# Seven products for up blocks 7, 8, 9, 11, 12, 13 and 14 of a fused transformer block, and one buffer each for gates and values

## The chip, the core and the metric

The kernel runs on one core of one Trainium2 chip. The metric is the device time of one execution, in microseconds (us). Blocks are counted from 0, as in the code.

## What is computed

One layer on a sequence of 512 tokens and 1024 features, in 32-bit floats: a normalisation, an mLSTM and a sparse attention side by side, an output projection, a feed-forward part with a short convolution, a gated embedding, and a last normalisation. The change touches the feed-forward part alone:

```python
def conv_ffn(h, w_up, conv_w, conv_b, w_down):
    u = h @ w_up                                   # 512x1024 by 1024x4096
    gate, val = jnp.split(u, 2, axis=-1)           # 2048 features each
    gate = conv(gate, conv_w) + conv_b             # three taps along the tokens, feature by feature
    return (jax.nn.silu(gate) * val) @ w_down      # 512x2048 by 2048x1024
...
x = x + conv_ffn(rms_norm(x, ln2_g[i]), w_up[i], conv_w[i], conv_b[i], w_down[i])
```

## The kernel before

Every product of 32-bit numbers is made of three: each operand is split into a high part (ScalarE copies it to the rounded type, line 205) and a low part (VectorE subtracts, line 209), and high by high, low by high and high by low are added up in PSUM. Names ending in `r`, `h` and `l` are the raw, high and low tile of one set of weights.

The 2048 features of the feed-forward part are 16 up blocks of 128. Features lie on the partitions, the 512 tokens along the free dimension. An **ordinary** block has two jobs, `wu80` (gate) and `wu81` (value): in each, eight slices of 128 input features by three products of 512 columns go into one bank. The gate is convolved (`convolve`, tile `cv`: one ScalarE and two VectorE instructions, then Silu), the value multiplied by it (tile `zv`), and the result split into `U` for the down products (`hidden`, lines 1224 and 1225).

A block in the table `FAST` takes the 2x2 product of gate and value halves by halves of the tokens and of the input features with seven half-sized products instead of eight. Its four jobs are `wu90`, `wu9s`, `wu9t` and `wu91`, with two, two, two and one of the seven products; each of these is twelve matmuls of 256 columns (`seven`, lines 1273 to 1277). What it needs beside them: GpSimd makes four sums of the raw weights (lines 1314 to 1318, in two rooms of the tile `ws`), which are split for jobs `s` and `t`; and VectorE adds the seven results together (lines 1340 to 1364, tiles `fu`, `fv`, `zg`, `zv`). The banks of such blocks change between two sets.

Weights are loaded on SyncE's queue and split by a stream of jobs: with `st.depth = 2` and `st.ahead = 3` two jobs are split and three more loaded ahead, in a ring of three raw, three high and three low tiles, so the high part of a job may be written only when TensorE has done the job three places before. The instructions of each engine run in the order of the program that a scheduler makes of these jobs. GpSimd's first sum for a block is put behind the latest clearing of a gate's margin:

```python
i = GE.tensor_add(s1, raw[:, 0:4], raw[:, 4:8])
behind(i, zeroed[0], "not long in front of its block")
GE.tensor_sub(s2, s1, r0[:, 0:4])
GE.tensor_sub(s3, r0[:, 0:4], raw[:, 0:4])
GE.tensor_sub(s4, r0[:, 4:8], s2)
```

Before, blocks 7, 9, 10, 12 and 13 are in the table; 8, 11, 14 and 15 are ordinary, and so are blocks 0 to 6. Blocks 0 to 4 are evacuated with the norm's factors (`rb2`) while the scaled input is made (`scaled_input`, with GpSimd sums of its own, lines 1261 to 1264).

Of the kernel before, what the change touches and what calls it, by code (L numbers as in the profile page):

```python
# [7 lines left out]
F32 = mybir.dt.float32  # L8
I32 = mybir.dt.int32
F32R = mybir.dt.float32r  # L10
# [5 lines left out]
S = 512  # L16
# [25 lines left out]
T_QK = 2.0  # L42
T_NR = 3.2
LASTW = 256
FAST = (7, 9, 10, 12, 13)
UNSCALED = 5
T_XN = 0.4, 4.9
T_TS = 2.0, 4.5
# [25 lines left out]
def f32(ap):  # L74
    return ap.bitcast(F32)
# [3 lines left out]
def hybrid_block_kernel(ctx: ExitStack, tc: tile.TileContext, a, out):  # L79
# [26 lines left out]
    def pV(name):  # L106
        return bank("V", 1, 1, name)
# [7 lines left out]
    def t2k(name, dt=F32):  # L115
        return tmp.tile([128, 512], dt, tag="t2k", name=name)
# [102 lines left out]
    def behind(later, sooner, why, wait=False):  # L219
        kind = mybir.DependencyClass.Sync if wait else mybir.DependencyClass.NoSync  # L220
        tc.add_manual_dep(later.ins, sooner.ins.name, mybir.DependencyInfo(kind, mybir.DependencyReason.DATA),
                          reason=why)
# [955 lines left out]
    def start_norm(norm, acc, name):  # L1178
        def stats():
            if norm is n3:  # L1180
                norm["yc"] = rstd_stats(acc, name)
                return
            ah, al = (fpool.tile([128, S], F32R, tag="zv", name=name + c) for c in "hl")
            SE.activation(ah, acc, AF.Copy)
            VE.tensor_sub(al, acc, f32(ah))
            st.after(T_NR, lambda: rows(ah, al))

        def rows(ah, al):

            ps = pV(name + "ps")  # L1190
            TE.matmul(ps, onesr, ah, start=True, stop=False)
            TE.matmul(ps, onesr, al, start=False, stop=True)
            v, y = t2k(name + "v"), t2k(name + "y")
            rb = tmp.tile([128, 512], F32, tag="rb", bufs=1, name=name + "rb")
            VE.tensor_scalar(v, ps, 1.0 / D, EPS, op0=ALU.mult, op1=ALU.add)
            SE.activation(y, v, AF.Abs_reciprocal_sqrt)
            VE.tensor_mul(rb, y, y)
            VE.scalar_tensor_tensor(rb, rb, -0.5, v, op0=ALU.mult, op1=ALU.mult)
            VE.scalar_tensor_tensor(rb, rb, 1.5, y, op0=ALU.add, op1=ALU.mult)
            norm["rb"] = rb  # L1200
            for fn in norm.get("pending", []):
                fn()
            for q, b in enumerate((0, 4, 1, 5, 2, 6, 3, 7)):
                st.after(T_XN[0] + T_XN[1] * q, lambda b=b: scaled_input(b))
        st.after(T_NS, stats)

    def gate_rows(f):
        zg = fpool.tile([128, S + 2], F32, name=f"zg{f}", tag="zg")
        zeroed[0] = GE.memset(zg[:, 0:2], 0.0)  # L1209
        return zg  # L1210

    def convolve(f, zg):
        cw = lambda j: cols[:, C_CW + 16 * j + f:C_CW + 16 * j + f + 1]
        cv = fpool.tile([128, S], F32, name=f"cv{f}", tag="cv")
        SE.activation(cv, zg[:, 2:S + 2], AF.Identity, scale=cw(2), bias=cols[:, C_CB + f:C_CB + f + 1])  # L1215
        VE.scalar_tensor_tensor(cv, zg[:, 1:S + 1], cw(1), cv, op0=ALU.mult, op1=ALU.add)  # L1216
        VE.scalar_tensor_tensor(cv, zg[:, 0:S], cw(0), cv, op0=ALU.mult, op1=ALU.add)  # L1217
        SE.activation(cv, cv, AF.Silu)  # L1218
        n2["cv"] = cv

    def hidden(f, zv):
        if f == max(FAST):
            U.room(range(f, 16), main.tile([128, 2, 4, S], F32R, tag="XH", name="u3"))
        SE.activation(U[0][:, f], zv, AF.Copy)  # L1224
        VE.tensor_sub(U[1][:, f], zv, f32(U[0][:, f]))  # L1225

    def up_evac(f, part, ps, rb2):

        if part == 0:
            zg = gate_rows(f)  # L1230
            if rb2 is None:
                SE.activation(zg[:, 2:S + 2], ps, AF.Copy)
            else:
                VE.tensor_mul(zg[:, 2:S + 2], ps, rb2)  # L1234
            convolve(f, zg)
        else:
            zv = fpool.tile([128, S], F32, name=f"zv{f}", tag="zv")
            if rb2 is None:
                VE.tensor_mul(zv, ps, n2["cv"])
            else:  # L1240
                VE.tensor_mul(zv, ps, rb2)
                VE.tensor_mul(zv, zv, n2["cv"])  # L1242
            hidden(f, zv)
# [53 lines left out]
    def up_fast(f):  # L1297
        d = {}
        half = lambda w, q: (w[0][:, 4 * q:4 * q + 4], w[1][:, 4 * q:4 * q + 4])

        def landed_a(raw):
            d["r0"] = raw

        def landed_b(raw):
            r0, d["r1"] = d["r0"], raw
            if not rooms:
                rooms.append(fpool.tile([128, 2, 8, 128], F32, bufs=1, name="ws", tag="xturn"))
                rooms.append(0)
            sums = []
            for _ in range(2):  # L1310
                sums.append(rooms[0][:, rooms[1] % 2])
                rooms[1] += 1
            s2, s1, s3, s4 = sums[0][:, 0:4], sums[0][:, 4:8], sums[1][:, 0:4], sums[1][:, 4:8]
# [5 lines that stand above are left out]
            d["sums"] = sums  # L1319

        def prep_b(name, raw, shape):
            return split(name, d["sums"][0], shape)

        def prep_c(name, raw, shape):
            return split(name, d["sums"][1], shape)

        def prep_d(name, raw, shape):
            return split(name, d["r1"][:, 4:8], shape)

        def run_a(wh, wl):  # L1330
            d["ps"] = fast_banks(f)
            d["u"] = t2k(f"fu{f}")
            d["v"] = t2k(f"fv{f}")
            p1, p2 = d["ps"][0:2]
            yield from seven(p1, half((wh, wl), 0), quarter(0, 0))
            v1 = d["v"][:, H:]
            yield from seven(p2, half((wh, wl), 1), quarter(4, 0))
            SE.activation(v1, p1, AF.Copy)
            d["zg"] = gate_rows(f)
            VE.tensor_add(d["zg"][:, 2:2 + H], p2, v1)  # L1340

        def run_b(wh, wl):
            p1, p2, p6, p5 = d["ps"][0:4]
            u2, u4 = d["u"][:, 0:H], d["v"][:, 0:H]
            yield from seven(p6, half((wh, wl), 0), tsum(1))
            yield from seven(p5, half((wh, wl), 1), tsum(0))
            VE.tensor_add(u2, p6, d["v"][:, H:])
            VE.tensor_add(u4, p5, u2)

        def run_c(wh, wl):  # L1350
            p5, p7, p3 = d["ps"][3:6]
            u2, u3, u4 = d["u"][:, 0:H], d["u"][:, H:], d["v"][:, 0:H]
            d["zv"] = fpool.tile([128, S], F32, name=f"zv{f}", tag="zv")
            yield from seven(p7, half((wh, wl), 0), tsum(2))
            yield from seven(p3, half((wh, wl), 1), quarter(4, H))
            VE.tensor_add(d["zg"][:, 2 + H:], p3, u4)
            convolve(f, d["zg"])
            VE.tensor_add(u3, p7, u2)
            VE.tensor_add(d["zv"][:, H:], p5, u3)

        def run_d(wh, wl):
            zv, p4 = d["zv"], d["ps"][6]
            yield from seven(p4, (wh, wl), tsum(3))
            VE.tensor_add(zv[:, 0:H], p4, d["u"][:, H:])
            VE.tensor_mul(zv, zv, n2["cv"])
            hidden(f, zv)

        full = [128, KB, 128]
        st.add(f"wu{f}0", a["w_up"][:, f, 0], full, run_a, landed=landed_a)
        st.add(f"wu{f}s", a["w_up"][:, f, 1], full, run_b, prep_b, landed_b)  # L1370
        st.add(f"wu{f}t", None, full, run_c, prep_c)
        st.add(f"wu{f}1", None, [128, 4, 128], run_d, prep_d)

# [33 lines left out]
    for f in range(16):  # L1407
        if f in FAST:
            up_fast(f)
# [5 lines left out]
    fpool = ctx.enter_context(tc.tile_pool(name="fpool", bufs=2))  # L1415
    U = Parts()
# [9 lines left out]
    for j in range(4):  # L1426
        st.after(T_TS[0] + T_TS[1] * j, lambda j=j: split_sums(j))
    st.until(f"wu{min(FAST) - 2}1")
    st.depth, st.ahead = 2, AHEAD
    st.until("wu71")  # L1430
    U.room(range(8, 12), main.tile([128, 2, 4, S], F32R, tag="B16", bufs=3, name="u2"))
    U.room((12,), fpool.tile([128, 2, 1, S], F32R, bufs=1, name="u12"))
    st.until(f"wu{max(FAST)}1")
    st.depth, st.ahead = 1, 0
    st.until("wu151")
# [114 lines left out]
    for t in range(NT):  # L1550
# [3 lines left out]
        for part, (c0, c1) in enumerate(cuts):  # L1554
            if part:
                ps = pG("pg1last")
            for k in range(KB):
# [5 lines left out]
                if part == 0 and k == 5:  # L1563
                    VE.tensor_mul(xo[:, t, 0], xo[:, t, 0], gF[:, 0])
                    f = 1.0 if t < NT - 1 else -0.5
# [101 lines left out]
```

## Time and profile before

| | |
|---|---|
| median of 3 runs | 622.81 us (622.48 to 622.87) |
| the profiled execution, its own time | 622.97 us |
| its span, first to last instruction | 621.2 us |
| TensorE (PE) busy | 609.9 us, 98% |
| VectorE (DVE) busy | 452.3 us, 73% |
| ScalarE (ACT) busy | 338.9 us, 55% |
| GpSimd (POOL) busy | 113.4 us, 18% |

Busy shares are averages over stages that differ; the up blocks in question lie between 386.9 and 480.9 us. The two digits rows of the page say how busy an engine is in 40 slices of some 15.5 us each.

### The profile page before, as it was taken

What the parts mean: (1) busy time and instruction counts of PE and PEld (TensorE: products, weight loads), DVE (VectorE), ACT (ScalarE), POOL (GpSimd) and SP (SyncE); (2) the same over time, 40 slices, a digit from 0 to 9 for tenths busy, and PEclk for the clock granted to TensorE, in tenths of its full rate; (3) what the DMA queues carried; (4) which work ended last, traced back from release to release, by engine and by line L of the source; (5) the groups of instructions that cost most, each with busy time, mean ns of one, the idle gap of its engine ahead of it and who ended that gap; (6) DMA issues with size and microseconds to landing.
All of it is one profiled execution on the core that took longest, in us unless ns stands there. A gap on an engine that the chain in (4) does not pass through costs nothing.

```text
span 621.2 us, 8920 instructions
## 1 busy us (share of the span) xinstructions
PE 609.9 (98%) x3195; PEld 505.1 (81%) x3195; DVE 452.3 (73%) x842; ACT 338.9 (55%) x700; POOL 113.4 (18%) x169
## 2 busy tenths in 40 slices
PE   8999999999999999999999999999999999999994
PEld 6888877777777778887878888999998888888784
DVE  5988847787877778883879997979794435355376
ACT  7556556777767766654656564554563223242254
POOL 0400009332333500000003624253500000000000
PEclk9999999999999999999999999999999999999998
DMA  8722035212211233022232332423232332634703
GB/s 309 284 74 85 19 118 144 61 35 68 70 43 60 77 128 102 35 59 79 69 102 88 108 109 102 137 72 132 78 127 68 102 100 78 161 102 145 192 4 135
DMA packets 23212, 63.07 MB, mean 102 GB/s; under 512 B 2744, under 2 KB 7736, under 8 KB 23100
## 3 DMA queue, kind: packets, MB, share of 16 engines
q1 hardware_dynamic: 21632, 59.93, 29.8%
q0 software_dynamic: 1248, 2.16, 1.5%
q8 instruction: 25, 0.41, 0.3%
q10 hardware_dynamic: 288, 0.41, 0.2%
q14 instruction: 19, 0.16, 0.1%
HBM read 56.72 MB, written 2.10 MB: 95 GB/s over the span
## 4 chain that ended last, share of the span: by engine, by line
PE 85%; DVE 8%; ACT 3%; issue 2%; DMA 2%; SPq 0%; POOL 0%; ACTq 0%; DVEq 0%; POOLq 0%
PE pu L496 6%; PE pu L495 6%; PE pu L499 6%; PE pd L499 5%; PE pd L496 5%; PE pd L495 5%; PE pt L894 2%; PE ptm L442 2%; PE pv L902 2%; PE pmq L495 1%; PE mo L1087 1%; PE pc L446 1%; PE pmq L499 1%; PE pmq L496 1%; PE pv L904 1%
## 5 line engine op out<-in xcount | busy, mean ns | idle before, releaser
L869 POOL TENSOR_SCALAR E<-E,rr,sg 128x512 f32<-128x512 f32 (+3 forms) x54 | 38.6, 714 | 71.3 <-DVE rr L864 53.2
L898 DVE TENSOR_TENSOR pl<-pt,ph 128x512 fp32r<-128x512 f32 x40 | 27.2, 687 | 7.5 <-ACT ph L897 6.9
L897 ACT ACTIVATE ph<-pt 128x512 fp32r<-128x512 f32 x40 | 23.6, 599 | 15.3 <-PE pt L894 13.9
L1571 POOL TENSOR_SCALAR vlast<-ss,ve 128x1 f32<-128x1 f32 x1 | 0.7, 728 | 151.2 <-ACT sq L1469 151.2
L894 PE MATMUL pt<-cols,E 128*128 128x128 f32 x160 | 26.4, 274 | 0.5 <-DVE E L869 0.4
L1209 POOL MEMSET zg<- 128x2 f32 x16 | 1.5, 100 | 137.3 <-DVE wu00l L209 92.4
L1398 DVE TENSOR_TENSOR X<-pd,X 128x512 f32<-128x512 f32 x8 | 5.5, 691 | 28.5 <-PE pd L499 28.5
L894 PEld LDWEIGHTS pt<-cols,E 128*128 128x128 f32 x160 | 20.0, 140 | 6.1 <-DVE E L869 0.7
L1218 ACT ACTIVATE cv<-cv 128x512 f32<-128x512 f32 x16 | 10.1, 633 | 25.7 <-DVE cv L1217 25.7
L862 ACT ACTIVATE E<-s,nm 128x384 f32<-128x384 f32 (+2 forms) x48 | 22.1, 470 | 0.0
L902 PE MATMUL pv<-ph,V 128*128 128x512 f32 x40 | 18.9, 472 | 0.0
L864 DVE RECIPROCAL rr<-rs 128x3 f32<-128x3 f32 x32 | 5.5, 171 | 16.6 <-ACT E L862 16.6
L1224 ACT ACTIVATE u<-zv 128x512 fp32r<-128x512 f32 x16 | 10.0, 626 | 12.5 <-DVE zv L1242 5.7
L1225 DVE TENSOR_TENSOR u<-zv,u 128x512 fp32r<-128x512 f32 x16 | 11.1, 694 | 7.8 <-ACT u L1224 7.8
L904 PE MATMUL pv<-pl,V 128*128 128x512 f32 x40 | 16.4, 410 | 0.1
L852 DVE TENSOR_REDUCE nm<-s 128x2 f32<-128x768 f32 (+2 forms) x24 | 16.3, 680 | 0.0
L527 POOL DMA_DIRECT2D Q<-hlq x12 | 6.3, 540 | 54.9 <-ACT hlq L522 54.9
L1215 ACT ACTIVATE cv<-zg,cols 128x512 f32<-128x512 f32 x16 | 13.1, 817 | 4.4 <-DVE zg L1234 2.2
L332 DVE TENSOR_TENSOR acc<-acc,sq 128x512 f32<-128x512 f32 x21 | 14.3, 683 | 0.1
L862 ACT ACTIVATE Ec<-s,nm 128x32 f32<-128x32 f32 x24 | 6.8, 282 | 11.9 <-DVE nm L852 8.7
L1216 DVE SCALAR_TENSOR_TENSOR cv<-zg,cols,cv 128x512 f32<-128x512 f32 x16 | 13.0, 812 | 0.3 <-ACT cv L1215 0.3
L1217 DVE SCALAR_TENSOR_TENSOR cv<-zg,cols,cv 128x512 f32<-128x512 f32 x16 | 12.4, 775 | 0.2
(1330 smaller groups left out, 2190.0 us busy)
## 6 DMA issues: line engine op xcount, KB each, us to landing
X<-in_xg SPq DMA_DIRECT2D x1, 2048.0 KB, 8.7
xo<-xturn SPq DMA_DIRECT2D x32, 64.0 KB, 2.1
wgr<-in_w_pg SPq DMA_DIRECT2D x4, 512.0 KB, 4.0
s1r<-in_w_s SPq DMA_DIRECT2D x3, 676.0 KB, 9.4
xT<-in_xg SPq DMA_DIRECT2D x3, 514.0 KB, 8.4
rawx<-in_w_mv SPq DMA_DIRECT2D x3, 512.0 KB, 7.5
Q<-hlq POOLq DMA_DIRECT2D x12, 128.0 KB, 2.9
out_y<-xo SPq DMA_DIRECT2D x3, 512.0 KB, 2.6
```

Of the source, the lines that this page charges most:

```text
L332: return VE.tensor_add(acc[:, :n], acc[:, :n], sq[:, :n])
L495: TE.matmul(ps, wh[:, w], rh[:, x, n], start=first and j == 0, stop=False)
L496: TE.matmul(ps, wh[:, w], rl[:, x, n], start=False, stop=False)
L499: TE.matmul(ps, wl[:, w], rh[:, x, n], start=False, stop=last and j == len(kx) - 1)
L852: VE.tensor_reduce(out=nm[:, 1:3], in_=sw, axis=AX.X, op=ALU.max, negate=True)
L862: SE.activation(e, p, AF.Exp, bias=nm[:, b:b + 1], accum_out=rs[:, b:b + 1])
L869: eng.tensor_scalar(e, e, rr[:, b:b + 1], sg[:, i, 3 * h + b:3 * h + b + 1], op0=ALU.mult, op1=ALU.mult)
L894: TE.transpose(pt[:, r * 128:(r + 1) * 128], Es[r][:, c0:c0 + 128], ident)
L897: SE.activation(ph, pt, AF.Copy)
L898: VE.tensor_sub(pl, pt, f32(ph))
L902: TE.matmul(pv, vs, ph, start=first, stop=False)
L904: TE.matmul(pv, vs, pl, start=False, stop=last)
```

## The change

Blocks 8, 11 and 14 join the table and block 10 leaves it, so that seven of the nine blocks from 7 on have seven products, in a run of three (7, 8, 9), one ordinary block (10), a run of four (11 to 14) and the ordinary block 15. The tiles `cv` and `zv` have one buffer each instead of two, the norm's two parts take one each of them, and the freed room holds the results `u12` and `u13` (the largest number in `FAST` is now 14, so the room that opens behind the last fast block holds 14 and 15).

```diff
-FAST = (7, 9, 10, 12, 13)
+FAST = (7, 8, 9, 11, 12, 13, 14)
...
-            ah, al = (fpool.tile([128, S], F32R, tag="zv", name=name + c) for c in "hl")
+            ah, al = (fpool.tile([128, S], F32R, tag=tag, bufs=1, name=name + c) for c, tag in (("h", "zv"), ("l", "cv")))
...
-        cv = fpool.tile([128, S], F32, name=f"cv{f}", tag="cv")
+        cv = fpool.tile([128, S], F32, name=f"cv{f}", tag="cv", bufs=1)
...
-            zv = fpool.tile([128, S], F32, name=f"zv{f}", tag="zv")
+            zv = fpool.tile([128, S], F32, name=f"zv{f}", tag="zv", bufs=1)
...
-            d["zv"] = fpool.tile([128, S], F32, name=f"zv{f}", tag="zv")
+            d["zv"] = fpool.tile([128, S], F32, name=f"zv{f}", tag="zv", bufs=1)
...
-    U.room((12,), fpool.tile([128, 2, 1, S], F32R, bufs=1, name="u12"))
+    for f in range(12, max(FAST)):
+        U.room((f,), fpool.tile([128, 2, 1, S], F32R, bufs=1, name=f"u{f}"))
```

On VectorE, the rows before the change in which block 7 ends and the ordinary block 8 is evacuated (`wu8..l` and `wu9..l` are low parts of weights, `pfa` to `pfd` and `pu` are PSUM banks, the last number of a name is a buffer's):

```order
L209 TENSOR_TENSOR wu90l_4203<-wu90r_4109,wu90h_4202 128x1024
L1365 TENSOR_TENSOR zv7_4147<-zv7_4147,cv7_4173 128x512
L1225 TENSOR_TENSOR u1_3454<-zv7_4147,u1_3454 128x512
L209 TENSOR_TENSOR wu9sl_4240<-ws_3988,wu9sh_4239 128x1024
L1216 SCALAR_TENSOR_TENSOR cv8_4234<-zg8_4231,cols_73,cv8_4234 128x512
L1217 SCALAR_TENSOR_TENSOR cv8_4234<-zg8_4231,cols_73,cv8_4234 128x512
L1239 TENSOR_TENSOR zv8_4270<-pu81_4245,cv8_4234 128x512
L209 TENSOR_TENSOR wu9tl_4275<-ws_3988,wu9th_4274 128x1024
```

At the same place now, from block 8's third job to the first low part for block 9:

```order
L209 TENSOR_TENSOR wu8tl_4202<-ws_3988,wu8th_4201 128x1024
L1365 TENSOR_TENSOR zv7_4143<-zv7_4143,cv7_4169 128x512
L1340 TENSOR_TENSOR zg8_4241<-pfa8_4211,fv8_4215 128x256
L209 TENSOR_TENSOR wu81l_4245<-wu8sr_4069,wu81h_4244 128x512
L1225 TENSOR_TENSOR u1_3454<-zv7_4143,u1_3454 128x512
L1347 TENSOR_TENSOR fu8_4214<-pfb8_4212,fv8_4215 128x256
L209 TENSOR_TENSOR wu90l_4275<-wu90r_4180,wu90h_4274 128x1024
```

The low part `wu90l` moves from before the multiplication of block 7's values to behind block 8's own splits and adds; where an ordinary block's six rows (two low parts, two taps, the multiplication, the result's split) stood between two fast blocks, the fifteen of a fast block stand (three whole low parts and a half one, seven adds, two taps, a multiplication and a split).

On GpSimd, the sums before the change at the place behind block 7's:

```order
L1209 MEMSET zg8_4231 128x2
L1314 TENSOR_TENSOR ws_3988<-wu9sr_4141 128x512
L1317 TENSOR_TENSOR ws_3988<-wu90r_4109,wu9sr_4141 128x512
L1316 TENSOR_TENSOR ws_3988<-ws_3988,wu90r_4109 128x512
L1209 MEMSET zg9_4314 128x2
L1318 TENSOR_TENSOR ws_3988<-wu90r_4109,ws_3988 128x512
```

And the same place now:

```order
L1209 MEMSET zg8_4241 128x2
L1314 TENSOR_TENSOR ws_3988<-wu8sr_4069 128x512
L1316 TENSOR_TENSOR ws_3988<-ws_3988,wu80r_4032 128x512
L1317 TENSOR_TENSOR ws_3988<-wu80r_4032,wu8sr_4069 128x512
L1318 TENSOR_TENSOR ws_3988<-wu80r_4032,ws_3988 128x512
L1314 TENSOR_TENSOR ws_3988<-wu9sr_4205 128x512
L1316 TENSOR_TENSOR ws_3988<-ws_3988,wu90r_4180 128x512
L1209 MEMSET zg9_4370 128x2
```

Four sums for block 8 have come in, and those for block 9 follow at once, with no ordinary block between them; the same holds for blocks 12, 13 and 14.

## Rows read from the trace of the kernel before

**Rows 1.** The page: TensorE's busy time, VectorE's busy tenths in 40 slices.

```profile
PE 609.9 (98%) x3195; PEld 505.1 (81%) x3195; DVE 452.3 (73%) x842; ACT 338.9 (55%) x700; POOL 113.4 (18%) x169
...
DVE  5988847787877778883879997979794435355376
```

**Rows 2.** Busy us of PE, PEld, DVE, ACT, POOL; blocks 8, 9, 10.

```profile
397.00:407.90 10.90, 10.90 (x50) 9.02 (x49) 8.10 (x9) 5.01 (x7) 6.56 (x5) 1.00 0.34 108
407.90:418.00 10.10, 10.10 (x86) 10.09 (x85) 9.07 (x12) 5.02 (x8) 6.03 (x5) 1.00 0.21 75
418.00:428.10 10.10, 10.10 (x87) 10.10 (x86) 10.00 (x19) 6.47 (x9) 0.10 (x1) 1.00 0.42 134
```

**Rows 3.** TensorE in order of time: start, us, instruction; first matmuls of blocks.

```profile
397.00 0.40 PE L495 MATMUL pu<-xnh,wu80h 128*128 128x512 f32 x1
...
407.91 0.28 PE L1273 MATMUL pfa<-xnh,wu90h 128*128 128x256 f32 x1
...
417.98 0.28 PE L1273 MATMUL pfa<-xnh,wu100h 128*128 128x256 f32 x1
...
418.94 0.64 PE L1277 MATMUL pfa<-xnh,wu100l 128*128 128x256 f32 x4
...
428.06 0.40 PE L495 MATMUL pu<-xnh,wu110h 128*128 128x512 f32 x1
```

**Rows 4.** VectorE in order of time, blocks 9 and 10.

```profile
411.53 1.96 DVE L209 TENSOR_TENSOR wu9tl<-ws,wu9th 128x1024 fp32r<-128x1024 f32 x1 [0.26 <-ACT wu9th L205]
...
414.01 1.78 DVE L209 TENSOR_TENSOR wu91l<-wu9sr,wu91h 128x512 fp32r<-128x512 f32 x1
415.71 0.41 DVE L1340 TENSOR_TENSOR zg<-pfa,fv 128x256 f32<-128x256 f32 x1
...
416.83 1.22 DVE L209 TENSOR_TENSOR wu100l<-wu100r,wu100h 128x1024 fp32r<-128x1024 f32 x1
...
421.75 1.21 DVE L209 TENSOR_TENSOR wu10tl<-ws,wu10th 128x1024 fp32r<-128x1024 f32 x1
...
423.82 0.68 DVE L209 TENSOR_TENSOR wu101l<-wu10sr,wu101h 128x512 fp32r<-128x512 f32 x1
...
425.35 1.21 DVE L209 TENSOR_TENSOR wu110l<-wu110r,wu110h 128x1024 fp32r<-128x1024 f32 x1
426.49 0.41 DVE L1348 TENSOR_TENSOR fv<-pfb,fu 128x256 f32<-128x256 f32 x1
```

**Rows 5.** GpSimd in order of time: the four sums for block 10.

```profile
409.72 1.32 POOL L1314 TENSOR_TENSOR ws<-wu10sr 128x512 f32<-128x512 f32 x1 [3.39 <-DMA wu10sr<-in_w_up]
411.11 1.29 POOL L1316 TENSOR_TENSOR ws<-ws,wu100r 128x512 f32<-128x512 f32 x1
...
413.56 1.68 POOL L1317 TENSOR_TENSOR ws<-wu100r,wu10sr 128x512 f32<-128x512 f32 x1 [1.12 <-DVE wu9tl L209]
415.20 1.74 POOL L1318 TENSOR_TENSOR ws<-wu100r,ws 128x512 f32<-128x512 f32 x1
```

**Rows 6.** VectorE in order of time, block 7.

```profile
391.57 1.22 DVE L209 TENSOR_TENSOR wu7tl<-ws,wu7th 128x1024 fp32r<-128x1024 f32 x1
...
395.03 1.22 DVE L209 TENSOR_TENSOR wu80l<-wu80r,wu80h 128x1024 fp32r<-128x1024 f32 x1
```

**Rows 7.** SyncE's queue: two loads of weights.

```profile
387.67 0.33 SPq L196 DMA_DIRECT2D wu81r<-in_w_up  x1
...
406.36 0.33 SPq L196 DMA_DIRECT2D wu10sr<-in_w_up  x1
```

**Rows 8.** ScalarE, VectorE and TensorE in order of time, blocks 1 and 3.

```profile
331.42 0.82 ACT L1215 ACTIVATE cv<-zg,cols 128x512 f32<-128x512 f32 x1
...
332.61 1.23 DVE L1242 TENSOR_TENSOR zv<-zv,cv 128x512 f32<-128x512 f32 x1
...
344.95 1.21 DVE L209 TENSOR_TENSOR wu30l<-wu30r,wu30h 128x1024 fp32r<-128x1024 f32 x1
...
347.03 1.30 PE L499 MATMUL pu<-x2h,wu30l 128*128 128x512 f32 x5
```

## Prediction

> **What bounds the kernel now.** I read the page first: TensorE is busy for 609.9 of 621.2 us, and VectorE, at 73% on the whole, reaches 9 tenths and more in seven slices, six of them between the 22nd and the 30th, where the up blocks lie [rows 1]. So a saving has to come out of TensorE's own work, unless another engine is pushed past it. The busy times block by block tell which one could be: in the ordinary block 8 VectorE works 8.10 of 10.90 us, in the fast block 9 9.07 of 10.10, in the fast block 10 10.00 of 10.10 [rows 2]. TensorE is dense in all of them. The second of two fast blocks already has a full VectorE, and the reader should keep that in mind: the change makes runs of three and four.
>
> **What TensorE gains.** Block 9 runs from 407.91 to 417.98 and block 10 to 428.06 [rows 3]: 10.07 and 10.08 us for 84 matmuls of 256 columns, 0.120 each. The ordinary block 8 runs from 397.00 to 407.91, 10.91 us for 48 matmuls of 512 columns, 0.227 each [rows 3]. An eighth less arithmetic is thus worth 0.83 us a block, because a half-sized matmul costs more than half. Three blocks become fast and one ordinary, so two net: **-1.65 us**. The Trainium skill ("TensorE: Matmul & The Clock Gate", section "Wait — 56ns, not 53.3ns?") has a warm matmul at its columns over 2.4 GHz plus some 2.5 ns; by that two blocks would be worth 2.35 us (an estimate from that page). The rows are slower at both sizes, and more so at 256, so the measured 0.83 stands.
>
> **What VectorE has to do for a fast block.** Between the starts of the low parts `wu100l` (416.83) and `wu110l` (425.35), where GpSimd has next to nothing to do (0.10 us in block 10, rows 2), VectorE runs fourteen of a fast block's fifteen rows; the fifteenth, an add of 0.41 us, stands behind at 426.49; records overlap by 0.04 to 0.08 us (`wu91l` ends at 415.79, the add behind it starts at 415.71), so it takes 0.34 of VectorE's time [rows 4]. That is 8.52 + 0.34 = **8.86 us**, against TensorE's 10.08. Undisturbed, VectorE keeps up with 1.22 us to spare.
>
> **What GpSimd does to it.** Four sums are made for each fast block, while the block before it runs. Rows 5 and 4 laid over each other show that they and VectorE's instructions exclude each other. The sum of 411.11 (1.29 us, 1.23 without the overlap) is running when `wu9tl` begins at 411.53: that split takes 1.96 us, while the like `wu10tl` at 421.75 takes 1.21. The sum of 413.56 is running when the half split `wu91l` begins at 414.01: 1.78 against the 0.68 of `wu101l` at 423.82. But the add at 415.71, which reads PSUM, keeps its 0.41 us beside the sum of 415.20. Hence a sum takes 1.23 us from VectorE where splits, taps or multiplications stand, and nothing where it lies beside an add from PSUM. The Trainium skill says the same ("SBUF — State Buffer", section "Who interferes with whom"): a VectorE instruction with two SBUF inputs and a GpSimd one that reads SBUF block each other for the whole instruction, one with at most one SBUF input does not. By that rule the change runs into a wall, and these rows agree with it.
>
> In the step from block 9 to 10, two of the four sums cost something: 0.75 + 1.10 = 1.85 us. The first, at 409.72, was over before `wu9tl`, ahead of which VectorE even rested for 0.26 us, and the last lay beside adds from PSUM. That is a start behind an ordinary block, in which VectorE rests. Inside a run it doesn't rest: in the new order, the stretch from `wu8tl` to `wu90l` holds four rows with SBUF operands (split, multiplication, half split, result) and two single adds between them, and GpSimd's four sums come in that stretch, each at its turn. Four sums are 4 x 1.23 = 4.9 us; I take off 0.34 each for the add of block 7's values just ahead and the one inside that a sum can lie beside, and some 0.1 at each of four hand-overs, where records overlap: **3.9 us** a step. The bounds are 1.85 (as measured behind an ordinary block) and 4.9 (nothing hidden).
>
> A step from fast to fast with sums then takes VectorE 8.86 + 3.9 = 12.8 us, TensorE 10.08: VectorE falls 2.7 us behind, and when its cover is used up TensorE waits for low parts.
>
> **How much cover there is.** TensorE uses a low part after eight matmuls of the high one. `wu100l` ends at 416.83 + 1.22 = 418.05, its first use is at 418.94 [rows 3, 4]: 0.9 us, with 1.85 already paid. `wu80l` ends at 395.03 + 1.22 = 396.25 [rows 6]; if block 8 is fast, it is wanted at 397.00 + 8 x 0.12 = 397.96: 1.7 us, with nothing paid, since no sums are made during block 7 now.
>
> The five steps:
> - 7 to 8: the second half of block 8's weights is loaded where `wu81r` was (387.67); with the 3.36 us that the like load took from 406.36 to its first sum at 409.72 [rows 5, 7], sums begin at 391.0 and run into `wu7tl` (391.57, rows 6) and the two rows with SBUF operands behind it, the last beside adds. Three sums, some 2.8 us, less 1.7 of cover: 1.1 us of waiting.
> - 8 to 9: no cover is left, 2.7 us.
> - 11 to 12, behind the ordinary block 10: as 9 to 10 is now, 0; 0.9 of cover remains.
> - 12 to 13: 2.7 - 0.9 = 1.8 us.
> - 13 to 14: 2.7 us.
>
> Behind 9 and 14 comes an ordinary block without sums, and VectorE's 8.86 us let it recover. Sum of waits: **+8.3 us**.
>
> **The rest.** One buffer for `cv`: before, block 1's first tap on ScalarE starts at 331.42, ahead of the multiplication that reads block 0's gate until 332.61 + 1.23 [rows 8]. Now it must wait for that, 2.4 us, and VectorE's tap behind it stands one place later; the swap with a scaling of the input fills most of it. The tightest use nearby is `wu30l`: it ends at 344.95 + 1.21 = 346.16 and is used at 347.03 [rows 8], so up to 0.9 us of delay costs nothing. Cost between 0 and 2.4 - 0.9 = 1.5 us; I take 0, as other rows stand ready on VectorE. `zv` and the norm's parts are read long before they are written again: 0. The four splits, the loads (3.36 us each until the sum can start, by the like one above) and the extra copies on ScalarE (5.0 to 6.5 of 10.1 us busy, rows 2) lie beside TensorE; without that cover a split on ScalarE would cost about what one costs VectorE, 1.21 us [rows 4].
>
> Sum against the profiled execution: 622.97 - 1.65 + 8.3 = 629.6; the runs' median, 622.81, is 0.16 lower, so **629.4 us**, 1.1% slower.
>
> **The rivals.**
> - *It does what it says: faster.* If each step's sums cost VectorE no more than its spare 1.22 us, no wait arises and the time is 622.81 - 1.65 = 621.2. That needs three of four sums beside adds or in idle time in every run; for it speaks that a wait of TensorE gives VectorE rest, against it the 1.85 of the best placed step. Chance 0.10.
> - *The sums cost in a run what they cost in the pair,* 1.85 us: a step takes 10.7, 0.63 over. Waits are 0.15, 0.63, 0, 0 and 0.36 us, 1.1 together: 622.3, no change that can be told. The rows for it are those of the pair; against it, VectorE's rest ahead of `wu9tl` [rows 4], of which a run has none. Chance 0.12.
> - *Nothing is hidden:* a step takes 13.8 us, 3.7 over. Waits 4.9 - 1.7 = 3.2, 3.7, 3.1 - 0.9 = 2.2, 3.7, 3.7 = 16.5, less 1.65: 637.7. Adds from PSUM that do run beside sums (415.71) speak against it. Chance 0.06.
>
> **How the numbers follow.** The forecast's own case, sums that cost between about 2.6 and 4.3 us a step, has 0.72 and spans 625 to 633. What a measurement can tell from no change is 0.2%, 1.25 us. Faster by more holds the first rival, 0.10; within it nearly all of the second, 0.11; slower the rest, 0.79. The range of 8 in 10 reaches from 623.8, the edge of the second rival, to 633.0.
>
> **What would show it.** Right: in the profile after, TensorE has waits of 1 to 2 us on VectorE before the low parts of blocks 8, 9, 13 and 14 (`wu80l`, `wu90l`, `wu130l`, `wu140l`), fast blocks of 11 to 13 us there, and of 10.1 in block 12; splits of 1.9 us and half splits of 1.7 beside GpSimd's sums; the stretch of blocks 7 to 15 grows from 94 to about 100.6 us, with the down products' part as before. Wrong: fast blocks of 10.1 us in all runs (the first rival), the waits where TensorE needs a bank or a loaded tile instead of a low part, or a wait before block 5 (one buffer too few).

## The result and the profile after

The changed kernel takes 628.03 us at the median of 6 runs (626.64 to 630.01), the kernel before 622.84 (622.48 to 623.88): a ratio of 1.0083, interval 1.0069 to 1.0097. It is slower by 5.2 us; 6.6 were forecast. The profiled execution took 628.76 us, with a span of 627.0.

The page after, with the rows that answer to [rows 1], and the shares of the chain that ended last:

```profile
PE 611.1 (97%) x3267; PEld 509.3 (81%) x3267; DVE 468.8 (75%) x860; ACT 341.0 (54%) x704; POOL 132.4 (21%) x177
...
DVE  6988757787777878873979996997998334445476
...
PE 68%; DVE 20%; issue 5%; ACT 4%; DMA 1%; POOL 1%; SPq 0%; ACTq 0%; DVEq 0%; POOLq 0%
```

Busy shares on the whole hardly moved; the chain did. Before, 85% of it was TensorE's and 8% VectorE's. The place shows in the busy times by block (PE, PEld, DVE, ACT, POOL, then the granted clock), which answer to [rows 2]; blocks 8, 9, 12 and 14:

```profile
397.00:407.90 10.90, 10.34 (x86) 10.13 (x85) 10.87 (x17) 5.61 (x8) 6.00 (x5) 1.00 0.41 113
407.90:419.10 11.20, 10.35 (x87) 10.15 (x86) 11.10 (x18) 5.99 (x9) 3.17 (x3) 1.00 0.35 104
...
441.00:451.00 10.00, 10.00 (x85) 10.00 (x85) 10.00 (x15) 5.83 (x8) 5.75 (x4) 1.00 0.42 125
...
462.00:476.00 14.00, 11.77 (x85) 11.56 (x85) 13.76 (x22) 6.62 (x10) 2.26 (x3) 0.88 0.39 114
```

In blocks 8 and 9 VectorE is busy throughout and TensorE has half a microsecond and more of holes; block 12 is dense on both; block 14 takes 14 us, and its clock is 0.88. What TensorE waited for between 380 and 490 us (total us, times, longest):

```profile
PE pfa L1277 <- DVE wu140l L209: 2.2, 1, 2.2
PE pfa L1277 <- DVE wu90l L209: 0.8, 1, 0.8
PE pfa L1277 <- DVE wu80l L209: 0.6, 1, 0.6
PE pfa L1273 <- DVE zg L1340: 0.5, 1, 0.5
PE pfa L1277 <- DVE wu130l L209: 0.4, 1, 0.4
PE pfc L1277 <- DVE wu7tl L209: 0.3, 1, 0.3
PE pfd L1277 <- DVE wu71l L209: 0.3, 1, 0.3
```

None of these waits was there before. Six are for low parts that VectorE makes, one is for a bank (`zg`). In TensorE's order of time they look so; compare [rows 3]:

```profile
397.02 0.28 PE L1273 MATMUL pfa<-xnh,wu80h 128*128 128x256 f32 x1
...
398.69 0.74 PE L1277 MATMUL pfa<-xnh,wu80l 128*128 128x256 f32 x4 [0.56 <-DVE wu80l L209]
...
407.91 0.28 PE L1273 MATMUL pfa<-xnh,wu90h 128*128 128x256 f32 x1
...
409.88 0.74 PE L1277 MATMUL pfa<-xnh,wu90l 128*128 128x256 f32 x4 [0.85 <-DVE wu90l L209]
...
439.42 0.39 PE L1273 MATMUL pfa<-th,wu111h 128*128 128x256 f32 x1 [0.46 <-DVE zg L1340]
...
462.78 0.28 PE L1274 MATMUL pfa<-xnl,wu140h 128*128 128x256 f32 x1
465.30 1.14 PE L1277 MATMUL pfa<-xnh,wu140l 128*128 128x256 f32 x4 [2.23 <-DVE wu140l L209]
466.23 0.41 PE L1273 MATMUL pfa<-xnh,wu140h 128*128 128x256 f32 x1
466.44 0.41 PE L1274 MATMUL pfa<-xnl,wu140h 128*128 128x256 f32 x1
...
468.79 0.31 PE L1273 MATMUL pfb<-th,wu14sh 128*128 128x256 f32 x1
...
476.00 0.40 PE L495 MATMUL pu<-xnh,wu150h 128*128 128x512 f32 x1
```

The low matmuls of block 9 start 1.97 us after the block's first instead of 0.96. Behind the wait of 2.23 us in block 14 the matmuls are 0.21 us apart, not 0.12.

From start to start, blocks 7 to 15 now take 11.12, 10.89, 11.18, 10.91, 10.95, 10.08, 10.92, 14.05 and 10.91 us. Together that is 385.90 to 486.91, 101.01 us, against 93.98 before (386.93 to 480.91): +7.03, where 6.65 were forecast. Blocks 2 to 6 take 10.88 each in both traces. Block 7 starts 1.03 us earlier in this execution, and the first rows that differ stand in the first 25 us of the program; so the span grew by 5.8 only.

VectorE in order of time, first the step from block 8 to 9, then from 11 to 12 and from 13 to 14; this answers to [rows 4]:

```profile
402.34 1.22 DVE L209 TENSOR_TENSOR wu8tl<-ws,wu8th 128x1024 fp32r<-128x1024 f32 x1
403.48 0.69 DVE L1365 TENSOR_TENSOR zv<-zv,cv 128x512 f32<-128x512 f32 x1
404.08 0.42 DVE L1340 TENSOR_TENSOR zg<-pfa,fv 128x256 f32<-128x256 f32 x1
404.42 1.47 DVE L209 TENSOR_TENSOR wu81l<-wu8sr,wu81h 128x512 fp32r<-128x512 f32 x1
405.80 1.78 DVE L1225 TENSOR_TENSOR u<-zv,u 128x512 fp32r<-128x512 f32 x1
...
407.84 1.99 DVE L209 TENSOR_TENSOR wu90l<-wu90r,wu90h 128x1024 fp32r<-128x1024 f32 x1
...
437.26 1.77 DVE L209 TENSOR_TENSOR wu111l<-wu11sr,wu111h 128x512 fp32r<-128x512 f32 x1
438.95 0.41 DVE L1340 TENSOR_TENSOR zg<-pfa,fv 128x256 f32<-128x256 f32 x1
...
450.48 1.98 DVE L209 TENSOR_TENSOR wu130l<-wu130r,wu130h 128x1024 fp32r<-128x1024 f32 x1
...
457.83 1.78 DVE L1365 TENSOR_TENSOR zv<-zv,cv 128x512 f32<-128x512 f32 x1
...
459.87 1.45 DVE L209 TENSOR_TENSOR wu131l<-wu13sr,wu131h 128x512 fp32r<-128x512 f32 x1
461.25 1.79 DVE L1225 TENSOR_TENSOR u<-zv,u 128x512 fp32r<-128x512 f32 x1
...
463.29 1.95 DVE L209 TENSOR_TENSOR wu140l<-wu140r,wu140h 128x1024 fp32r<-128x1024 f32 x1
```

And GpSimd's sums for block 9, with the first one for block 14; this answers to [rows 5]:

```profile
402.36 2.97 POOL L1314 TENSOR_TENSOR ws<-wu9sr 128x512 f32<-128x512 f32 x1 [4.82 <-DMA wu9sr<-in_w_up]
405.41 1.63 POOL L1316 TENSOR_TENSOR ws<-ws,wu90r 128x512 f32<-128x512 f32 x1
...
407.03 1.71 POOL L1317 TENSOR_TENSOR ws<-wu90r,wu9sr 128x512 f32<-128x512 f32 x1
408.70 2.27 POOL L1318 TENSOR_TENSOR ws<-wu90r,ws 128x512 f32<-128x512 f32 x1
...
457.32 1.74 POOL L1314 TENSOR_TENSOR ws<-wu14sr 128x512 f32<-128x512 f32 x1 [3.72 <-DMA wu14sr<-in_w_up]
```

The two lists read together show where VectorE's time goes. A half split that takes 0.68 us alone takes 1.45 to 1.78 where a sum is in its way, a result's split or a multiplication 1.78 instead of 0.68, a whole split 1.95 to 2.19 instead of 1.22 (2.19 is `wu11tl`'s). And it is VectorE that is late, not a load or a sum: `wu80l`, `wu90l`, `wu130l` and `wu140l` are made from loaded weights and from no sum, and ahead of each of them VectorE's rows follow one another for 5 us and more without a hole of 0.1 us. The pieces that the sums took from VectorE add up, step by step, to 3.06 us (7 to 8), 2.66 (8 to 9), 2.06 (11 to 12), 2.63 (12 to 13) and 3.71 (13 to 14).

### The profile page after: what moved, and what is told of

Its sections match the earlier page's. It is cut to its first block, busy times and chain, and to the rows that moved or that the text cites. A ratio compares the mean times of both kernels' runs of the same rounds, so it can differ in the third digit from the quotient of the medians.

```text
span 627.0 us, 9106 instructions
## 1 busy us (share of the span) xinstructions
PE 611.1 (97%) x3267; PEld 509.3 (81%) x3267; DVE 468.8 (75%) x860; ACT 341.0 (54%) x704; POOL 132.4 (21%) x177
## 4 chain that ended last, share of the span: by engine, by line
PE 68%; DVE 20%; issue 5%; ACT 4%; DMA 1%; POOL 1%; SPq 0%; ACTq 0%; DVEq 0%; POOLq 0%
PE pd L495 5%; PE pd L499 5%; PE pd L496 5%; PE pt L894 2%; PE ptm L442 2%; PE pc L446 2%; DVE u L1225 2%; PE pv L902 2%; PE pmq L495 1%; PE mo L1087 1%; PE pmq L499 1%; PE pmq L496 1%; PE pv L904 1%; DVE cv L1216 1%; PE poa L495 1%
## 5 line engine op out<-in xcount | busy, mean ns | idle before, releaser
L1225 DVE TENSOR_TENSOR u<-zv,u 128x512 fp32r<-128x512 f32 x16 | 15.5, 968 | 3.9 <-ACT u L1224 3.9
```

## The experiments

The theory: GpSimd's four sums shut VectorE out, and in a run of fast blocks VectorE has no rest to make it good (the expectations call it the port theory). The rivals: the buffers that became single (buffer theory); a fast block's fifteen rows on VectorE, whatever GpSimd does (rows theory); loads or sums that come too late in themselves; TensorE's own products. Unless it says otherwise, an edit is one to the changed kernel.

**The buffers alone.** The old table with the rest of the change:

```diff
-FAST = (7, 8, 9, 11, 12, 13, 14)
+FAST = (7, 9, 10, 12, 13)
```

> The table of before (7, 9, 10, 12, 13) with all the rest of the change: one buffer each for gates and values, the norm's parts one in each. Port theory (GpSimd's sums shut VectorE's instructions with SBUF operands out, and in a run of fast blocks VectorE falls behind): no run is longer than before, so 622.8, within 0.6 us. Buffer theory (the single buffers make ScalarE and VectorE wait): most of the 5 us, 626 or more.

Measured: 623.25 us, ratio 1.0003 (0.9993 to 1.0012). The single buffers alone are not the cause: VectorE's, ScalarE's and GpSimd's instructions stand in the order of before in these blocks, and by the interval they cost at most 0.12%, 0.7 us. They are not quite free within the blocks, though: block 9 takes 10.60 us and block 12 10.46, where before it was 10.07, and the nine blocks 94.90 instead of 93.98. The one wait that the profile has for it, in block 9, and the GpSimd row:

```profile
PE pfa L1273 <- DVE zg L1340: 0.3, 1, 0.3
```

```profile
410.04 1.30 POOL L1314 TENSOR_TENSOR ws<-wu10sr 128x512 f32<-128x512 f32 x1 [3.90 <-DMA wu10sr<-in_w_up]
```

The first sum for block 10 starts 2.76 us after block 9 does (407.28), instead of 1.81 [rows 3, 5]. The sums now take 2.19 us from VectorE (1.10 from a result's split, 1.09 from the half split) instead of 1.85, and its rows stand 0.4 us later against the block; so the add from bank `pfa`, which TensorE needs free for the block's last product, comes 0.28 us too late. In the changed kernel the wait for a bank in block 11 stands at the same place, in the first fast block behind an ordinary one; how much of its 0.87 us is the buffers' was not separated. Why the load in front of the sum lands later wasn't settled.

**The sums cut to a sixteenth.** 8 of 128 columns of each sum are made (the first one shown, the others likewise), the rest of the room is zeroed once:

```diff
-            i = GE.tensor_add(s1, raw[:, 0:4], raw[:, 4:8])
+            cut = lambda t: t[:, :, 0:8]
+            i = GE.tensor_add(cut(s1), cut(raw[:, 0:4]), cut(raw[:, 4:8]))
```

> The changed kernel with GpSimd's four sums cut to 8 of 128 columns per slice (the rest of their room is zero, so jobs s and t multiply wrong weights); every instruction, its order and its waits stay. Port theory: the waits go, 622.8 - 1.65 = 621.2, up to 622 if some short wait stays; fast blocks of 10.1 us throughout. Rows theory (a fast block's fifteen rows are too much for VectorE in a run, whatever GpSimd does): 626 to 628 as changed. Buffer theory: 626 or more as well.

Measured: 620.50 us, ratio 0.9956 (0.9941 to 0.9971). TensorE waits for nothing, and all seven fast blocks take 10.07 or 10.08 us. A sum of this kernel, and the busy times over blocks 7 to 15:

```profile
398.32 0.25 POOL L1316 TENSOR_TENSOR ws<-wu9sr 128x32 f32<-128x32 f32 x1 [7.19 <-DMA wu9sr<-in_w_up]
```

```profile
386.68:479.03 92.35, 92.35 (x685) 88.57 (x684) 74.93 (x118) 49.76 (x68) 11.42 (x32) 1.00 0.35 103
```

92.35 us is 1.63 less than before's 93.98: the gain of the products as forecast (1.65), with nothing lost. From block 7 to 14 the instructions of VectorE, ScalarE and GpSimd stand in the order of the changed kernel, with the same buffers; only the length of the sums differs, and with it when things happen (the sum above starts 1.57 us into block 8, behind its load; in the changed kernel it is 5.34). So the sums' time on GpSimd decides, not the number of rows and not the buffers by themselves. Whether they act on VectorE or make a split wait for a late sum or load, this run alone doesn't tell; the changed kernel's VectorE rows above do, and the next two runs were meant to.

**More sums in the kernel before.** Two of the four made twice:

```diff
             GE.tensor_sub(s2, s1, r0[:, 0:4])
             GE.tensor_sub(s3, r0[:, 0:4], raw[:, 0:4])
+            GE.tensor_sub(s2, s1, r0[:, 0:4])
+            GE.tensor_sub(s3, r0[:, 0:4], raw[:, 0:4])
```

> The kernel before with two of the four sums of each fast block made twice by GpSimd (same results; 2.5 us more of GpSimd's time a block). Port theory: VectorE loses up to 2.5 us more in the steps 9 to 10 and 12 to 13, of which 0.4 to 0.9 us is covered: about 1.5 us of TensorE's waiting in each and up to 0.5 at block 7, 625.8 (624 to 628). Rows theory and buffer theory: GpSimd has time to spare, 622.8.

Measured: 632.67 us, ratio 1.0151 (1.0136 to 1.0166). The sign is right, the size far too small. The largest of its waits:

```profile
PE pfa L1273 <- DVE zg L1342: 2.0, 2, 1.5
PE pfc L1277 <- DVE wu9tl L209: 1.0, 1, 1.0
...
PE pfc L1273 <- ACT wu9th L205: 0.9, 1, 0.9
PE pfc L1273 <- ACT wu12th L205: 0.9, 1, 0.9
```

Two of them are for high parts that ScalarE copies out of a sum: here the sums themselves came too late, and blocks 9 and 12 took 14.92 and 14.16 us. The run mixes the slowed VectorE with a chain through GpSimd, which the changed kernel doesn't have (none of its waits above is for `ACT`), and so it settles nothing about the price of a sum to VectorE.

**The sums on VectorE.** The same four instructions, on the other engine, and the first no longer held behind a clearing of a gate's margin:

```diff
-            i = GE.tensor_add(s1, raw[:, 0:4], raw[:, 4:8])
-            behind(i, zeroed[0], "not long in front of its block")
-            GE.tensor_sub(s2, s1, r0[:, 0:4])
...
+            VE.tensor_add(s1, raw[:, 0:4], raw[:, 4:8])
+            VE.tensor_sub(s2, s1, r0[:, 0:4])
...
```

> The changed kernel with the four sums of each fast block on VectorE instead of GpSimd; all is computed. Port theory: the four take VectorE 4 x 0.60 = 2.4 us a step, while GpSimd's took 2.7 to 3.7 us of it in the steps within the runs of the changed kernel; 8.86 + 2.4 = 11.3 against TensorE's 10.08, 1.2 us over in each, with waits of some 0.7 + 1.2 + 0 + 0.9 + 1.2 = 4 us: 625 (623.5 to 626.5), below the changed kernel though VectorE has more rows. Rows theory (VectorE's own number of rows decides, GpSimd's sums are beside the point): slower than the changed kernel, 630 or more.

Measured: 620.87 us, ratio 0.9963 (0.9950 to 0.9977): faster than both kernels, and 4 us better than expected. Busy times of the nine blocks, and VectorE around a sum and at the low parts of blocks 12, 13 and 14:

```profile
386.00:480.00 94.00, 94.00 (x693) 89.94 (x692) 89.51 (x145) 51.11 (x70) 0.79 (x8) 1.00 0.36 107
```

```profile
434.85 1.22 DVE L209 TENSOR_TENSOR wu120l<-wu120r,wu120h 128x1024 fp32r<-128x1024 f32 x1
...
442.43 0.68 DVE L1314 TENSOR_TENSOR ws<-wu13sr 128x512 f32<-128x512 f32 x1
...
446.70 1.21 DVE L209 TENSOR_TENSOR wu130l<-wu130r,wu130h 128x1024 fp32r<-128x1024 f32 x1
...
457.97 1.21 DVE L209 TENSOR_TENSOR wu140l<-wu140r,wu140h 128x1024 fp32r<-128x1024 f32 x1
```

VectorE does a sum in 0.68 us (0.60 without the overlap); made by GpSimd, the same sum costs it up to 1.1. The step from 13 to 14 takes 11.27 us, just what 8.86 + 4 x 0.60 makes, 1.2 more than TensorE's. Still TensorE never waits: blocks 7 to 15 take 92.40 us. What the expectation got wrong is the cover. `wu120l` is done at 436.07 and wanted at 439.10, 3.0 us, not the 0.9 that it took from [rows 3, 4]: those 0.9 were left behind a step slowed by GpSimd's sums. The kernel with short sums, whose order is unchanged, has 3.1 us there (435.78 to 438.85). Here the step holds four sums too, but the scheduler ordered VectorE's other rows anew: the first tap of the ordinary block 10 starts 8.8 us into the block, in the changed kernel 12.3, and the rest of 2.8 us that VectorE has at the end of this block in the changed kernel is gone. The third step of the run uses the 3.0 us up; `wu130l` has 1.3 us left, and `wu140l`, done at 459.18, would have had 0.1 (block 14 would start at 458.30, its low matmuls at 459.26). The scheduler also put `wu140`'s first eight matmuls ahead of `wu131`'s product, which leaves more. So the 620.87 us are the move together with the order that it brought; what each is worth was not separated.

**The same move without the longer runs.** The old table, single buffers, sums on VectorE:

> The table of before (7, 9, 10, 12, 13), single buffers, and the sums on VectorE. Port theory: before, TensorE waits for nothing in these blocks, so there is nothing to win: 622.9 within 0.6 us, and VectorE's sums are worth something in longer runs alone. If the sums on VectorE are better by themselves (shorter than GpSimd's, so everything behind them earlier), 621.5 or less.

Measured: 622.32 us, ratio 0.9988 (0.9978 to 0.9997); the nine blocks take 93.98 us, as before. Beside the kernel before, that is a gain of 0.1% (0.0 to 0.2), and not in these blocks. The run that differs from it in the move alone (and in the order that comes with it) is the one with the single buffers (94.90 us, ratio 1.0003): beside that, the move takes away the 0.9 us that blocks 9 and 12 had lost. The large gain needs the longer runs.

**Pairs instead of runs.** One fast block more than before, and none behind two others:

```diff
-FAST = (7, 8, 9, 11, 12, 13, 14)
+FAST = (7, 8, 10, 11, 13, 14)
```

> The changed kernel with the table (7, 8, 10, 11, 13, 14): six fast blocks, three pairs, an ordinary block behind each. Port theory: 0.83 us of TensorE's work less than before; the step 7 to 8 costs 1.9 us as in the changed kernel (blocks 7 and 8 took 11.12 and 10.89 us there instead of 10.08), the steps 10 to 11 and 13 to 14 between 0 (as 9 to 10 before) and 0.9 (as 11 to 12 after): 624.8 (623.5 to 625.7). Rows theory: a pair is free, as it is before, so 622.0. Buffer theory: about 627.

Measured: 623.61 us, ratio 1.0009 (1.0000 to 1.0019). The pairs behind an ordinary block take 10.16 and 10.32, 10.07 and 10.11 us; the pair 7 and 8 takes 11.00 and 10.88, and that is where the waits are. Since blocks 2 to 6 leave VectorE time, the sums for block 7 ought to come earlier there:

```diff
-    st.until(f"wu{min(FAST) - 2}1")
+    st.until(f"wu{min(FAST) - 3}1")
```

> The three pairs (7, 8, 10, 11, 13, 14) with the deeper look-ahead of jobs set one block sooner, so that block 7's sums come earlier. Port theory: block 7 no longer starts its splits 1 us later than the other first blocks of a run, the 1.7 us that blocks 7 and 8 took over 10.08 in the pairs shrink to 0.5 or less: 623.6 - 1.2 to 1.7 = 622.2 (621.6 to 622.6), below both kernels. If block 7's waits come from something else (the banks, the load of block 8's second half), the time stays at 623.6.

Measured: 622.52 us, ratio 0.9989 (0.9981 to 0.9998). Block 7 is down to 10.07, block 8 to 10.61, and one wait is left:

```profile
PE pfa L1277 <- DVE wu80l L209: 0.3, 1, 0.3
```

**The same look-ahead with the full change.**

> The changed kernel with the deeper look-ahead set one block sooner. Port theory: only the first step gains, up to 1 us: 627 to 628. If the waits of all the runs come from loads and splits that start too late, the whole 5 us go: 623 or less.

Measured: 628.12 us, ratio 1.0072 (1.0055 to 1.0089), beside 1.0083 for the change itself. Blocks 7 and 8 come down to 10.07 and 10.63, but 9, 11, 13 and 14 stay at 11.17, 11.10, 10.91 and 14.04. So loads and sums that come late at the head of the first run account for 1.3 us of blocks 7 and 8, and not for the rest; in the time of the whole, 0.1 us above the expected range, the gain doesn't show.

**Without block 14.**

```diff
-FAST = (7, 8, 9, 11, 12, 13, 14)
+FAST = (7, 8, 9, 11, 12, 13)
```

> The changed kernel with block 14 ordinary again (7, 8, 9, 11, 12, 13): two runs of three. Port theory: blocks 7 to 13 as in the changed kernel, block 14 at 10.9 instead of 14.05 us (its wait of 2.2 us and the lower clock behind it gone): 625.0 (624 to 626). If the sums' price were the same for each fast block wherever it stands, block 14 would give back 5 / 5 steps = 1 us and cost 0.8: 627.8.

Measured: 626.42 us, ratio 1.0056 (1.0042 to 1.0070), 0.4 us above the range that the theory gave. Blocks 7 to 9 and 11 to 13 take 11.02, 10.90, 11.16, 11.11, 10.08 and 10.69 us, 4.48 over 10.08 in sum; one fast block more than before saves 0.83, and the difference, 3.65, is about what the nine blocks show (97.66 us instead of 93.98). Block 14 as a fast one thus costs 3.35 us between the two profiles, and by the ratios 0.27%, 1.7 us: the profiled execution of the changed kernel was 0.7 us above its median, and its blocks begin 0.87 us earlier than here. Dropping block 14 takes away the largest single delay and leaves more than half of the loss: the runs of three cost too, not the longest run alone.

## Why the prediction was right, step by step

The forecast was 629.4 us, slower, with the mechanism of GpSimd's sums. Time and sign came out, and the place but for block 11; the sum of the waits came out partly by luck.

- **TensorE's gain, -1.65 us.** Right: -1.63 in the kernel with short sums, where nothing waits. The estimate from the Trainium skill ("TensorE: Matmul & The Clock Gate", section "Wait — 56ns, not 53.3ns?") is not borne out; by that rule's figures it is 2.38, not the 2.35 that I wrote.
- **VectorE's clean step, 8.86 us.** Right: with the sums on VectorE, the step from 13 to 14 takes 11.27 us with four sums at 0.60, which leaves 8.87. In the changed kernel it takes 12.81 (450.48 to 463.29), of which 3.74 are the excess of its slowed rows; 9.07 are left.
- **The sums' price, 3.9 us a step.** Right for the last step (3.71), too high for the steps from 8 to 9 and 12 to 13 (2.66 and 2.63). (My subtraction makes 3.8, not 3.9: 4.9 less 0.68 and 0.4.) In those two the first sum did not get in at its turn: asked for at 402.36, it takes 2.97 us, while VectorE runs `wu8tl` and then the multiplication at full speed, and it starts with the add from PSUM at 404.08. I had counted one turn for each engine. The Trainium skill's rule ("SBUF — State Buffer", section "Who interferes with whom"), that two such instructions exclude each other whole and an add from PSUM does not take part, agrees with the rows shown here: the add of 404.08 keeps its 0.42 us beside the sum. Who goes next it puts down to the order of issue, and by these rows a sum already issued was overtaken.
- **The waits.** What each block took over 10.08 us, beside the forecast:

| block | forecast | measured | what made it |
|---|---|---|---|
| 7 and 8 | 1.1 | 1.04 + 0.81 | block 7's own low parts, then `wu80l` |
| 9 | 2.7 | 1.10 | a sum less in VectorE's way |
| 11 | 0 | 0.87 | bank of the last product, behind `zg` |
| 12 | 0 | 0 | |
| 13 | 1.8 | 0.84 | a sum less in VectorE's way |
| 14 | 2.7 | 2.40 + 1.57 | 1.57 of it a lower clock |
| sum | 8.3 | 8.63 | |

The sum is close because misses on both sides cancel, and that is luck: 2.44 of the 8.63 us, block 11's and the lower clock's, were in no term of the forecast. In blocks 7 and 8 the sums took 3.06 instead of 2.8, and I had looked at `wu80l` alone: block 7's own `wu7tl` and `wu71l` come late first, and all of block 7's 1.04 us are theirs. Block 7 also starts sooner behind its own last sum, 0.25 us (385.65 to 385.90) instead of 0.58 (386.35 to 386.93). The pairs (0.27), the kernel without block 14 (0.23) and the old table with single buffers (0.24) have the same, so by these profiles it goes with the rest of the change and is no accident of this execution. In block 11 I had looked for low parts only; the wait for a bank, named among the signs of being wrong, cost 0.72 us of the 0.87, and the old table with single buffers has a wait of this kind without any longer run. Before, there were 0.42 us to spare at this place (the add of 415.71 ends at 416.12, the matmul starts at 416.54).
- **The single buffers, 0 to 1.5 us, taken as 0.** Blocks 2 to 6 are as before, so the tap that must wait for the multiplication cost nothing. In the table of before they shift a sum and lengthen two blocks by 0.9 us together, by another way than the one I bounded; the time doesn't show it (1.0003). So some of the loss in blocks 7 and 11 may be theirs; with short sums they cost nothing.
- **The cover, 0.9 us behind an ordinary block.** In the changed kernel it is 0.6 (`wu120l` is done at 441.29 and wanted at 441.91), but it is no constant: with short sums and the same order it is 3.1.
- **The rivals.** That the change would do what it says (621.2 us) has its time with the sums out of the way: 620.50 and 620.87. Its condition, sums that VectorE doesn't feel, is not met where GpSimd makes them. No step had the price of the second rival (1.85 us; the least was 2.06) or of the third (4.9; the most was 3.71).

## What to carry to other kernels

Before a run of like stages is made longer, reckon the step of the second engine inside the run, without the rest that it has behind an ordinary stage; here 8.86 us of VectorE against 10.08 of TensorE looked like room, and four sums on a quiet third engine took it. Work handed to GpSimd is not free for VectorE where both read two SBUF operands: a sum of 128x512 cost VectorE up to 1.1 us as GpSimd's and 0.60 as its own, and moving the four sums over, with the order that the scheduler then made, turned +0.83% into -0.37%. And a cover is to be measured in the kernel that will have it, for it depends on what the step ahead of it costs.

## What the runs showed of the hardware that was not expected

Behind TensorE's wait of 2.23 us in block 14, its matmuls of 256 columns are 0.213 us apart, which is 1.2 GHz, until 468.79, and 0.12 again from 469.05. The granted clock of that stretch (busy times as above):

```profile
462.80:468.80 6.00, 3.77 (x20) 3.56 (x19) 5.90 (x10) 1.76 (x2) 1.36 (x1) 0.72 0.49 162
```

Sixteen matmuls took 3.49 us instead of 1.92: 1.57 us on top of the wait. (The first four behind each shorter wait take 0.10 us more too.) From 465.30 to 468.79 the granted clock is 0.52. After the waits of 0.3 to 0.9 us in the other blocks it stayed at 1.00. With the look-ahead the block takes 14.04 us again. But it doesn't take a wait that long: in the kernel with more sums, block 9 has waits of 0.24, 0.88 and 1.04 us within 6 us, and behind the third its matmuls stand 0.21 us apart too (granted clock 0.50 from 420.0 to 421.3, 0.89 over the block). Block 12 of that kernel, with waits of 0.88, 0.74 and 1.55 us, has 1.00. What sets the difference was not tried.

Of GpSimd's sums, those asked for at 402.36 and 445.18, 0.02 and 0.18 us after a split began, were passed by the next VectorE instruction as well (2.97 and 2.79 us), and the one at 457.32, 0.62 us after, was not (1.74). Whether the moment decides it was not tried.
